# Hybrid encoder layer: both merge gates as seven block products behind the heads, triangular inverses without DRAM, outputs of a head in a tile of their own, decays refilled step by step

## The chip, the cores and the metric

The kernel runs on one core of one Trainium2 chip. The metric is the device time of one execution in microseconds (us). Three runs of the kernel before gave 1963.44, 1961.55 and 1962.57 us. The profile is of one execution more; its times count from that execution's first instruction.

Engines are named as in the profile: PE is the matrix engine (PEld its weight loads), DVE the vector engine, ACT the scalar engine, POOL the engine GpSimd, SP the engine that issues nearly all DMAs. L332 is line 332 of the kernel before.

## The reference, cut to what matters

One layer over 1040 tokens (16 learned tokens ahead of 1024), width 1024, all in float32:

```python
h = rmsnorm(h_res, norm1_w)
proj = h @ w_in                                   # 9248 columns
(q, k, v, z, b_raw, a_raw, sc_b, sc_c, sc_x, gate_a, gate_b) = split(proj)
o_dn = gated_deltanet_bidir(q, k, v, z, b_raw, a_raw, ...)   # 8 heads, forward and backward scan
y_a = o_dn @ w_branch_dn
y_b = (sc_b * dwconv3(sc_c * sc_x)) @ w_branch_sc
merged = sigmoid(gate_a) * y_a + sigmoid(gate_b) * y_b
h_res += merged @ w_out
h_res += (silu(gu[:, :FF]) * gu[:, FF:]) @ w_down            # gu = rmsnorm(h_res) @ w_gate_up
out = rmsnorm(h_res)
```

A head of the delta net works on chunks of tokens. In each chunk and direction it needs the inverse of a unit triangular matrix (beta times k k^T times a decay), and then a recurrent step: the state S of 128x128 goes from chunk to chunk, forward in one direction, backward in the other.

## The kernel before, in words

**Matmuls.** Each float32 operand is split into a high and a low part (`split`, L85), and a product is three matmuls: high x high, high x low, low x high. A full product of w_in's 128 columns with all tokens ("a unit") is 48 matmuls with 512 columns each (two halves, eight k steps, three matmuls: `dense_steps`, L324), or 72 shorter ones in three pieces of 336 (or 322), 320 and 384 columns.

**The heads' stage.** Up to about 985 us, PE works through units: 24 for q, k, v of the eight heads, 8 for z, 24 for the short convolution (columns C, X, B; `u_short`, L417) and 7 for gate B (`u_gate`, L450). `pick` (L923) chooses the next: q, k, v first if `qkv_ok` allows, else the next of the list `fill_units`. A chosen unit runs two units later (list `ahead`), its weights are loaded and split meanwhile. `qkv_ok` (L919) holds a head back until `near` (a count that the scan of an earlier head raises when it starts step NEAR = 3) and `nscan` (scans begun) allow it. The first unit of a head, its k, waits in `u_qkv` (L378) after its first piece until the scan three heads before has ended (`freed`), since it takes that head's buffer.

**The streams.** Between the steps of the units, `run_streams` (L967) advances the generators of the heads' chain, and `pump` (L301) issues DVE work of four lanes (`conv`, `short`, `fs`, `norm`). All of it is one order written out ahead by a planner that keeps estimated clocks T of PE, DVE, ACT and POOL; the engines then run that order, each in order. For head h:

- `g_decay` (L514): one DMA broadcasts the head's row of decays into PQ (16 tiles of 128x128, two buffers), then a mask is added (L522) and ACT takes exponentials (L527). It may start when the scan of head h-2 has ended (`freed`).
- `g_norm` (L531): transposes and norms of q and k; then, when the scan of h-2 is wholly done (`done`, and `stored` some time after it), k k^T and q k^T for each chunk (L583), times the decays into NP (L613) and PQ (L617). NP has two buffers.
- `g_inv` (L623): the 32x32 diagonal blocks of NP go out to DRAM (nd, L641) and come back in another layout into fN (L653); `fs_job` (L484) inverts them by forward substitution, 62 DVE operations in a row (L491, L495); the result goes out to DRAM (pd, L671) and back into NP (L676). With the lock taken (`take`, L509), ACT copies and DVE transposes (L687 to L697) and matmuls of blocks follow (L706 to L741). The 16x16 matrix of the learned tokens is inverted meanwhile on POOL on one partition (L661).
- `g_scan` (L745): under the same lock it scales v (L764), and after the inverse 8 steps (L796 to L873). The outputs are gathered in parts of NP (`oacc`, L773), normalised, transposed and stored (L899, L902) after the lock is given back.

One lock serves the scan and the second part of the inverse. One generator of each kind runs at a time.

**Behind the heads.** `ph1.close()` frees the stage's memory, and the tiles of the next stage are allocated in it. One unit of gate B is made by `dense` (L1427), then gate A, the short convolution's projection and the delta net's projection each by `seven` (L1367): a product of 2x2 blocks by seven block products, each of 4 k steps, 4 tiles and 3 matmuls, so 7 x 48 = 336 matmuls (L1382) in place of 8 x 48 = 384. The sums of blocks of the hidden states (T1 to T4) are made late in the heads' stage (`block_sums`, L271) and kept in DRAM. The gates' tanh values go to DRAM (ta_d, tb_d) and come back at the merge.

**At the start.** POOL makes triangular masks (L1178 to L1196) in memory of their own while PE still makes the first units. The pool `dn` (L1298) takes over the memory of the start's pool `st`; `g_gates` (L1202) then uses the masks in PE matmuls (L1266, L1278).

## Time and profile before

| | us |
|---|---|
| median of three runs | 1962.57 |
| lowest, highest | 1961.55, 1963.44 |
| span of the profiled execution | 1959.4 |
| last matmul of the heads' stage begins (L332) | 985.2 |
| the one dense unit behind it | 985.4 to 996.5 |
| first matmul of `seven` (L1382) | 996.5 |
| output projection begins (L1596) | 1225.0 |
| gate and up projection begins (L1656) | 1318.4 |
| down projection begins (L1813) | 1742.0 |

The page gives for each engine its busy time and share of the span, then the span in 40 slices, then the chain of work that ended last, followed backwards. Further views group instructions by line (times in ns for one), print them in order of time, or sum them up over a stretch. A matmul's end is modelled, so the distance between the starts of matmuls, not their durations, tells the rate. An idle time in square brackets is followed by what ended it.

### The profile page before, as it was taken

The page shows a single profiled execution, that of the slowest core. Times are in us where ns is not written, and L with a number is a line of the kernel's source. Part 1 is how long each engine was busy: PE and PEld are TensorE (multiplying, and loading weights), DVE is VectorE, ACT ScalarE, POOL GpSimd, SP SyncE. Part 2 cuts the span into 40 slices and gives each one's busy share as a digit, 9 for nine tenths or more (in the row PEclk, how much of TensorE's full clock was granted, in tenths as well). Part 3 has the DMA queues.
Part 4 walks back from the last instruction along what each step waited for, and adds up shares of the span by engine and source line. Part 5 has one row for each costly group of instructions (what it writes and reads, how often), then busy time and mean ns, then how long its engine had stood idle before and what let it go on. Part 6 is the DMA issues. An engine that isn't in the chain of part 4 may idle for free.

```text
span 1959.4 us, 31938 instructions
## 1 busy us (share of the span) xinstructions
PE 1941.7 (99%) x11962; PEld 1704.4 (87%) x11962; DVE 1468.1 (75%) x2804; ACT 867.9 (44%) x2014; POOL 158.4 (8%) x457
## 2 busy tenths in 40 slices
PE   8999999999999999999999999999999999999998
PEld 8998899999899999998888888887888888888887
DVE  4778778788887888787358798559787887756574
ACT  5463544646455554533445545234232332324343
POOL 3012112020110202110000000000000000000001
PEclk9999999999999999999999999999999999999999
DMA  4222332323222222224386623332666644587654
GB/s 146 68 76 80 103 99 60 87 60 87 60 76 67 85 65 79 70 69 153 103 310 246 206 88 121 115 119 73 212 232 209 209 165 163 179 279 243 194 181 155
DMA packets 243136, 264.11 MB, mean 135 GB/s; under 512 B 46820, under 2 KB 166933, under 8 KB 240549
## 3 DMA queue, kind: packets, MB, share of 16 engines
q1 hardware_dynamic: 242981, 262.07, 42.1%
q8 instruction: 94, 1.54, 0.3%
q14 instruction: 61, 0.50, 0.1%
HBM read 189.58 MB, written 72.44 MB: 134 GB/s over the span
## 4 chain that ended last, share of the span: by engine, by line
PE 89%; DVE 5%; ACT 3%; issue 1%; DMA 1%; POOL 0%; SPq 0%; POOLq 0%; DVEq 0%; ACTq 0%
PE pm L332 31%; PE pm L1382 5%; PE pd L1382 4%; PE pe L1382 3%; PE pm L1656 3%; PE pm L1658 3%; PE pm L1657 2%; PE pd L1658 2%; PE pd L1656 2%; PE pd L1657 2%; PE pe L1658 2%; PE pe L1656 2%; PE pe L1657 2%; PE pm L1814 1%; PE pm L1815 1%; PE pm L1813 1%
## 5 line engine op out<-in xcount | busy, mean ns | idle before, releaser
L332 PE MATMUL pm<-hTh,wh 128*128 128x512 f32 (+4 forms) x1328 | 483.8, 365 | 0.1
L332 PE MATMUL pm<-hTh,wl 128*128 128x512 f32 (+4 forms) x1328 | 450.5, 340 | 0.0
L332 PE MATMUL pm<-al,wh 128*128 128x512 f32 (+4 forms) x1328 | 449.6, 339 | 0.5 <-DVE al L1047 0.5
L332 PEld LDWEIGHTS pm<-hTh,wl 128*128 128x128 f32 x1328 | 249.1, 188 | 15.5
L332 PEld LDWEIGHTS pm<-hTh,wh 128*128 128x128 f32 x1328 | 250.2, 189 | 13.6 <-ACT hTh L1041 0.2
L332 PEld LDWEIGHTS pm<-al,wh 128*128 128x128 f32 x1328 | 250.4, 189 | 12.9 <-DVE al L1047 0.7
L87 DVE TENSOR_TENSOR al<-raw,ring_h 128x1024 fp32r<-128x1024 f32 x73 | 88.4, 1223 | 63.6 <-ACT ring_h L86 63.2
L86 ACT CAST ring_h<-raw 128x1024 fp32r<-128x1024 f32 x73 | 76.9, 1054 | 109.7 <-PE pd L1815 35.3
L940 DVE TENSOR_TENSOR wl<-raw,wh 128x512 fp32r<-128x512 f32 x122 | 84.1, 690 | 32.0 <-ACT wh L943 27.1
L355 DVE SCALAR_TENSOR_TENSOR kq<-ra,wc,kq 128x520 f32<-128x520 f32 (+1 forms) x128 | 95.9, 749 | 2.3 <-ACT kq L389 1.2
L821 ACT ACTIVATE w<-pd,small 128x128 f32<-128x128 f32 x128 | 40.2, 365 | 124.9 <-PE pd L814 106.4
L128 POOL TENSOR_SCALAR ss<-ss 128x1 f32<-128x1 f32 x13 | 4.6, 353 | 951.1 <-ACT b L1825 603.4
L491 DVE TENSOR_TENSOR tm<-fP,fN 128x135 f32<-128x135 f32 (+23 forms) x248 | 72.1, 291 | 10.0 <-DMA fN<-nd 3.3
L495 DVE TENSOR_TENSOR fP<-fP,tm 128x135 f32<-128x135 f32 (+23 forms) x248 | 71.8, 289 | 7.3
L943 ACT CAST wh<-raw 128x512 fp32r<-128x512 f32 x122 | 74.8, 619 | 0.1
L87 DVE TENSOR_TENSOR raw<-pair,raw 128x1024 fp32r<-128x1024 f32 (+1 forms) x42 | 48.0, 1143 | 30.4 <-ACT raw L86 30.4
L86 ACT CAST raw<-pair 128x1024 fp32r<-128x1024 f32 (+1 forms) x42 | 41.7, 992 | 58.4 <-PE pd L1382 27.5
L87 DVE TENSOR_TENSOR wl<-pair,wh 128x1024 fp32r<-128x1024 f32 (+1 forms) x42 | 48.1, 1144 | 21.7 <-ACT wh L86 21.6
L86 ACT CAST wh<-pair 128x1024 fp32r<-128x1024 f32 (+1 forms) x42 | 41.7, 992 | 46.0 <-PE pd L1382 24.7
L843 DVE SCALAR_TENSOR_TENSOR S<-S,eGl,pd 128x128 f32<-128x128 f32 x104 | 31.8, 344 | 38.2 <-PE pd L831 30.8
L130 POOL TENSOR_TENSOR small<-small,minus_half 128x9 f32<-128x9 f32 x16 | 29.5, 1842 | 353.8 <-DVE small L878 264.0
L661 POOL TENSOR_TENSOR tm<-mP,mN 1x15 f32<-1x15 f32 (+7 forms) x120 | 37.3, 311 | 237.0 <-DMA mN<-ndm 228.7
(660 smaller groups left out, 4945.7 us busy)
## 6 DMA issues: line engine op xcount, KB each, us to landing
raw<-in_w_in_dram SPq DMA_DIRECT2D x64, 512.0 KB
raw<-in_w_gate_up_dram SPq DMA_DIRECT2D x44, 512.0 KB
sums<-in_w_down_dram SPq DMA_DIRECT2D x22, 512.0 KB
t_d<-sums SPq DMA_DIRECT2D x11, 1024.0 KB
raw<-s_d SPq DMA_DIRECT2D x44, 256.0 KB
raw<-t_d SPq DMA_DIRECT2D x44, 256.0 KB
act_d<-b SPq DMA_DIRECT2D x43, 256.0 KB
raw<-act_d SPq DMA_DIRECT2D x33, 256.0 KB
```

Source lines behind the costliest of these rows:

```text
L86: nc.scalar.copy(hi, src)
L87: nc.vector.tensor_tensor(out=lo, in0=src, in1=hi.bitcast(F32), op=ALU.subtract)
L332: mm(po[:, :n], (wl if j == 2 else wh)[:, k], xl[k][:, t0:t0 + n] if j == 1 else xh[k][:, t0:t0 + n], start=(i == 0), stop=(i == 3 * KT - 1))
L355: nc.vector.scalar_tensor_tensor(out=acc, in0=raw[:, h0 + t:h0 + t + hn], scalar=wc[:, t, col:col + 1], in1=acc, op0=ALU.mult, op1=ALU.add)
L491: nc.vector.tensor_tensor(out=tv, in0=fP[:, 0:r, j:j + 1].broadcast_to([P, r, n]), in1=fN[:, j:j + 1, j + 1:32].broadcast_to([P, r, n]), o ...
L495: nc.vector.tensor_tensor(out=fP[:, 0:r, j + 1:32], in0=fP[:, 0:r, j + 1:32], in1=tv, op=ALU.subtract)
L940: nc.vector.tensor_tensor(out=u[1][1][:, k], in0=u[2][:, k], in1=u[1][0][:, k].bitcast(F32), op=ALU.subtract)
L943: nc.scalar.copy(u[1][0][:, k], u[2][:, k])
L1382: mm(bank[t], a[:, c], b, start=fresh, stop=first and k == 3 and j == 2, skip_group_check=not first)
L1656: mm(po, ah[:, k], bhk, start=k == 0, stop=False)
L1657: mm(po, ah[:, k], blk, start=False, stop=False)
L1658: mm(po, al[:, k], bhk, start=False, stop=k == 3)
```

## The change

Both gates leave the heads' stage. Its fill list ends with seven of the eight B units of the short convolution; the eighth is made by `dense` behind the heads, in the place of gate B's eighth unit. Then `seven` runs for gate B and for gate A. So `seven` now runs four times. The results of the short convolution's taps (yc) go through DRAM to the late B units.

```diff
     fill_units += [(off + j * P, lambda w, j=j, i=i: u_short(j, i, w), None, i)
-                   for j in range(8) for i, off in enumerate((OSC, OSX, OSB))]
-    gates = [(j, off, d_[j]) for off, d_ in ((OGB, tb_d), (OGA, ta_d)) for j in range(8)]
-    late = gates[max(0, len(gates) - LATE):]
-    fill_units += [... u_gate(j, d_, w) ... for j, off, d_ in gates[:len(gates) - LATE]]
-    NEAR = 3
+                   for j in range(8) for i, off in enumerate((OSC, OSX))]
+    fill_units += [(OSB + j * P, lambda w, j=j: u_short(j, 2, w), None, None) for j in range(7)]
+    NEAR = 1
...
+    w = wload(w_in, OSB + 7 * P)
+    yc = s4(SEQ)
+    nc.sync.dma_start(yc, yc_d[7])
+    for i in range(2):
+        po = psany()
+        dense(po, w, hx, C0 + META + 512 * i, 512)
+        nc.vector.tensor_tensor(out=yc[:, halves[i]], in0=po, in1=yc[:, halves[i]], op=ALU.mult)
+        front.pop(0)()
+    nc.sync.dma_start(p_d[7], yc)
...
-    seven(ga, bank_m, bank_d, (0, 1), evict_ga, during_ga, ...)
+    for d, X, Y, dst, during in ((gb, bank_m, bank_d, tb_d, during_gb), (ga, bank_d, bank_m, ta_d, during_ga)):
+        seven(d, X, Y, (0, 1), evict_gate(dst), during, ...)
```

`during_gb` loads the blocks of w_in and T1 to T4 for gate A while gate B's products run, as `during_ga` does for the projection after it; the two sets of PSUM banks change places from one `seven` to the next.

The decays are refilled slot by slot. PQ and NP become two fixed tiles each; slot i of PQ holds the forward chunk i and the backward chunk 7 - i, the two that step i of the scan uses.

```diff
+        def fetch(i):
+            for d, c in enumerate((i, NC - 1 - i)):
+                nc.sync.dma_start(PQ[:, i, d], grow[h:h + 1, c, d].broadcast_to([P, P]))
+            return T["pe"] + ARRIVE          # ARRIVE is 5000 ns now, it was 10000
+        for i in range(NC + 1):
+            while i < NC and h > 1 and heads[h - 2]["steps"] <= i:
+                yield T["pe"] + 100
...
-        while done < h - 1 or "PQ" not in st_:
-        if h > 1:
-            yield heads[h - 2]["stored"]
+        while "PQ" not in st_:
+        order = (3, 4, 2, 5, 1, 6, 0, 7)     # chunks, as the slots that they need come free
...
-        oacc = [NP[:, c, c // 4] for c in range(NC)]
+        O = dn.tile([P, NC, P], F32, tag="o", name=uid("o"))
+        oacc = [O[:, c] for c in range(NC)]
...
-        if h < H and h < freed + 2 and not decs:
+        if h < H and h < freed + 3 and not decs and (h < 2 or "steps" in heads[h - 2]):
-        if ... h < freed + 3 and not norms and ...
+        if ... h < scaled_heads + 3 and not norms and ...
```

The inverse's blocks no longer go through DRAM. ACT copies them together (four copies of 32x512), two DVE transposes bring them into the layout of `fs_job` (256 and 1024 columns), and two more (512 columns each) bring the result back. The rows of a block are spread over two groups of partitions so that each operation of `fs_job` has j // 2 + 1 rows instead of up to 16. The copies of finished blocks into NP (`diag`, 32x256 on ACT) stand between the matmuls of the second part.

```diff
-            r = min(j + 1, 8) if j < 16 else 8 + min(j - 15, 8)
+            r = j // 2 + 1
...
+            nc.scalar.copy(E[B(b)].rearrange("p d c i -> p c d i"), NP[B(b), :, :, B(b)])     # for b in range(4)
+        nc.vector.transpose(E[:, 0], E[:, 0])
+        nc.vector.transpose(fN.rearrange("p i (s x) -> p i s x", s=2),
+                            E.rearrange("p d c i -> p i (d c)").unsqueeze(2).broadcast_to([P, 32, 2, 2 * NC]))
         job = enqueue("fs", fs_job(h, fN, fP))
...
+        nc.vector.transpose(Z.rearrange("p d c r -> p r (d c)"), fP.rearrange("p r (s x) -> p (r s) x", s=2))
+        nc.vector.transpose(W, Z)
         yield from take("inv")
```

The learned tokens' matrix gets a generator of its own, `g_meta`, on 16 partitions of POOL, begun as soon as the matrix is there; the scan waits for it (`learned`). The triangular masks of the start are now made in the first NP buffer, so behind the allocation of the pool `dn`, and `g_gates` puts its rows rr there too.

More of the change, by code (lines that the diff above doesn't have):

```diff
@@ L28 @@
 NF = FF // P
-LATE = 9
 EPS = 1e-6
@@ L179, in encoder_layer @@
     p_d = [dr.tile([P, SEQ], F32, name=f"p_d{i}") for i in range(KT)]
+    yc_d = [dr.tile([P, SEQ], F32, name=f"yc_d{i}") for i in range(KT)]
     ta_d = [dr.tile([P, SEQ], F32, name=f"ta_d{i}") for i in range(KT)]
@@ L654, in g_inv @@
[L654 to L665 removed]
+        fPf = fP.rearrange("p r i -> p (r i)")
@@ new lines, in g_inv @@
+        nc.gpsimd.memset(fP, 0.0)
+        nc.gpsimd.memset(fPf[:, 1:512:34], 1.0)
+        for b in range(4):
+            even = fPf[32 * b:32 * b + 16]
+            nc.gpsimd.memset(even[:, 1:512:34], 0.0)
+            nc.gpsimd.memset(even[:, 0:512:34], 1.0)
+        on("pool", 1500)
+        for b in range(4):
+            nc.scalar.copy(E[B(b)].rearrange("p d c i -> p c d i"), NP[B(b), :, :, B(b)])
+            A(512)
+        yield T["act"] + HOP
+        nc.vector.transpose(E[:, 0], E[:, 0])
@@ L767, in g_scan @@
         yield T["act"] + HOP - 1000
-        while not st_.get("inverted"):
+        while not (st_.get("inverted") and st_.get("learned")):
             yield T["pe"] + 100
@@ L952, in start_streams @@
         h = nnorm
-        if h < H and ndec and h < freed + 3 and not norms and all(k in heads[h] and heads[h][k]() for k in ("tk", "tq")):
+        if h < H and ndec and h < scaled_heads + 3 and not norms and all(k in heads[h] and heads[h][k]() for k in ("tk", "tq")):
             norms.append([g_norm(h, heads[h]), T["dve"] + HOP, h])
             nnorm += 1
+        h = nmeta
+        if h < H and not metas and heads[h].get("Nm_done"):
+            metas.append([g_meta(h, heads[h]), T["dve"] + HOP, h])
+            nmeta += 1
         h = ninv
@@ L1422, in encoder_layer @@
-    for j, off, dst in late[:len(late) - 8]:
-        w = wload(w_in, off + j * P)
-        th = s4(SEQ)
-        for i in range(2):
-            po = psany()
-            dense(po, w, hx, C0 + META + 512 * i, 512)
-            nc.scalar.activation(th[:, halves[i]], po, AF.Tanh, scale=0.5)
-            if front:
-                front.pop(0)()
-        nc.sync.dma_start(dst, th)
+    w_gate = {"a": w_in[:, OGA:OGA + D], "b": w_in[:, OGB:OGB + D]}
+    gb = {k: pair(t) for k, t in zip("ABCDEG", ("b0", "b1", "b2", "b3", "mB", "mA"))}
```

380 lines of the change are left out of this document (185 added, 195 removed).

## The prediction

> **What bounds the kernel now.** I began with the page's shares and slices, then summed the engines by stretch.
>
> ```profile
> span 1959.4 us, 31938 instructions
> PE 1941.7 (99%) x11962; PEld 1704.4 (87%) x11962; DVE 1468.1 (75%) x2804; ACT 867.9 (44%) x2014; POOL 158.4 (8%) x457
> PEclk9999999999999999999999999999999999999999
> 30.00:985.00 955.00, 951.09 (x7475) 882.62 (x7476) 740.27 (x1883) 481.06 (x1513) 131.45 (x402) 1.00 0.28 80
> 997.00:1226.00 229.00, 229.00 (x1010) 189.24 (x1009) 189.86 (x206) 117.61 (x145) 0.00 (x0) 1.00 0.57 196
> ```
>
> The last two rows are stretches: length, then busy us of PE, PEld, DVE, ACT and POOL, granted clock, DMA share, GB/s. The first is the heads' stage, the second the three runs of `seven`. PE is without work for 4 us of 955 in the one and for none in the other, at full clock. So PE's queue bounds both, and an edit counts by the matmuls that it takes out and by the waits that it puts into PE's order. The rate, from the chain that ended last (start, length, what):
>
> ```profile
> 996.47 2.04 PE pm L1382 x9
> 1018.23 2.04 PE pm L1382 x9
> L455 ACT ACTIVATE rb<-pm x14: 578/598/617, 892.1 to 985.7; 128x512 f32<-128x512 f32 x14
> L741 ACT COPY NP<-pd x8: 581/582/584, 211.2 to 901.0; 64x512 f32<-64x512 f32 x8
> ```
>
> Two block products, 96 matmuls, lie between the first two rows: 21.76 / 96 = 0.2267 us for a matmul of 512 columns. L455 evicts gate B's units, two halves each: seven units stand at the very end of the heads' stage. L741 ends a head's inverse, and its first and last start give (901.0 - 211.2) / 7 = 98.5 us per head. So the heads' chain, not PE, sets how early the stage could end if its fill were taken away, and that is what the change does. Here is one turn of this chain, from the end of head 5's scan to that of head 7:
>
> ```profile
> 765.43 0.60 PE L834 MATMUL pd<-v,PQ 128*128 128x128 f32 x4
> 800.66 0.69 ACT L527 ACTIVATE PQ<-PQ,negG 128x128 f32<-128x128 f32 x2
> 816.77 0.42 DVE L617 TENSOR_TENSOR PQ<-pe,PQ 128x256 f32<-128x256 f32 x1
> 820.01 1.83 DVE L639 STREAM_TRANSPOSE NP<-NP 32x256 f32<-32x256 f32 x4
> 836.94 0.18 DVE L491 TENSOR_TENSOR tm<-fP,fN 128x31 f32<-128x31 f32 x1
> 872.37 0.19 DVE L495 TENSOR_TENSOR fP<-fP,tm 128x16 f32<-128x16 f32 x1
> 885.47 0.41 ACT L687 COPY Xe<-NP 32x256 f32<-32x256 f32 x1 [2.97 <-DMA meta_inv<-pdm]
> 901.02 0.58 ACT L741 COPY NP<-pd 64x512 f32<-64x512 f32 x1
> L777 PE MATMUL pd<-vS,meta_inv x16: 270/273/275, 214.7 to 903.9; 128*128 128x128 f32 x16
> 903.84 0.38 PE L777 MATMUL pd<-vS,meta_inv 128*128 128x128 f32 x2
> 961.57 0.60 PE L834 MATMUL pd<-v,PQ 128*128 128x128 f32 x4
> ```
>
> The decays take 35 us after scan 5 (to 801.3), the products 16 (817.2), the way out through DRAM and back 15 (821.8 to 836.9), the substitution 35.6, the second way through DRAM 12.9 (872.6 to 885.5), the inverse's second part 16.1 (to 901.6), the scan 58.3 (903.8 to 962.2). That is 196 us for two heads, 98 for one, and agrees with L741.
>
> **Gate B's matmuls.** A dense gate is 8 x 48 = 384 matmuls of 512 columns, `seven` 336. 48 go: 48 x 0.2267 = **-10.9 us**. The eight units that leave the heads' stage (seven of gate B, the eighth B unit) are 8 x 48 x 0.2267 = 87.1 us, the new `seven` is 336 x 0.2267 = 76.2 us, and the dense unit between stays. PE's work of the heads' stage then ends at 985 - 87.1 = 898 us. The -10.9 holds only if the chain is done by then; from 898 each us of lateness is a us lost, and at 908.8 nothing is left.
>
> **The chain after.** With slots fetched as scan h-2 steps, about 12 us are left behind its last step: one fetch (5 us by the planner), mask and exponentials 1.1, two chunks' products about 2 (rows L527, L617), hops. The first DRAM way becomes four ACT copies (0.58 each by L741) and two transposes (0.46 by L639's mean for 256 columns, perhaps 1.3 for 1024), some 6 us; the second becomes two transposes and hops, some 3. These shapes are not in the trace; were each as dear as the whole of what it replaces, 15 and 13 us would stay. The substitution keeps 62 operations with 24% fewer elements, 2856 in place of 3752 in a pass:
>
> ```profile
> L491 DVE TENSOR_TENSOR tm<-fP,fN 128x135 f32<-128x135 f32 (+23 forms) x248 | 72.1, 291 | 10.0 <-DMA fN<-nd 3.3
> L495 DVE TENSOR_TENSOR fP<-fP,tm 128x135 f32<-128x135 f32 (+23 forms) x248 | 71.8, 289 | 7.3
> L940 DVE TENSOR_TENSOR wl<-raw,wh 128x512 fp32r<-128x512 f32 x122 | 84.1, 690 | 32.0 <-ACT wh L943 27.1
> 500.00:600.00 100.00, 100.00 (x833) 95.75 (x833) 88.22 (x231) 53.30 (x176) 16.90 (x53) 1.00 0.26 72
> ```
>
> At 1.07 ns an element (L617's 256 columns take 0.42 us, L491's 31 take 0.18) that is about 1.9 us of 18 per head; say 33 us for the 35.6. The second part loses seven transposes and gains copies beside matmuls: 14 for 16.1. The turn is then 12 + 6 + 33 + 3 + 14 + 58 = 126, 63 per head. But the second part and the scan share the lock: 14 + 58 + some 8 for vS and hand-overs = **80 us a head**, and this binds. Head 0's first scan starts near 198 (L777's first start is 214.7; less two DRAM ways of some 10, plus the 3 below); its end is near 255, that of head 7 at 255 + 7 x 80 = 815, its outputs stored at 827. PE's 898 comes 71 us later: the period may be 90 before PE waits. DVE can stretch it. In the densest stretch (last row) it has 88.2 of 100 us. In the stage it falls from 740 us by 8 x 1.38 (units' splits, two of L940 each), 8 x 1.9 (substitution) and about 8 x 1.7 (11 transposes of 0.46 against four of 3.3 in all) to some 700 in 868, 81%, but nearer 90 until the chain ends. So I take 84 to 86 as likely, an end near 860, and count the chain at nothing. What covers it is the B units' work after 860; with that cover gone it costs what the rival below says.
>
> **The start.** The masks move behind the allocation of `dn`.
>
> ```profile
> 37.88 0.20 POOL L1178 MEMSET Uf<- 128x128 f32 x1
> 43.32 0.30 POOL L1196 TENSOR_SCALAR mask<-Ub 128x128 f32<-128x128 f32 x1
> 53.43 0.35 POOL L1301 MEMSET meta_inv<- 128x128 f32 x2 [9.82 <-PE pe L1053]
> 54.55 0.37 ACT L1223 COPY scratch<-pe 128x256 f32<-128x256 f32 x1 [0.67 <-PE pe L83]
> 54.95 0.42 DVE L1227 TENSOR_TENSOR scratch<-pe,scratch 128x256 f32<-128x256 f32 x1 [3.44 <-ACT scratch L1223]
> 71.42 0.51 DVE L1258 TENSOR_TENSOR scratch<-scratch,alg 128x64 f32<-128x64 f32 x4
> 73.29 0.34 PE L1266 MATMUL pe<-scratch,U2f 128*128 128x72 f32 x2
> ```
>
> POOL spends 5.7 us on them (37.9 to 43.6) while nothing waits. The first memset in `dn` could start only at 53.4, when PE had read the last tile of `st`. The masks now go ahead of it in POOL's order, and the memset of scratch that L1223 overwrites comes behind: L1223 moves from 54.5 to about 60.2. Queued behind it on ACT are a split of weights and the eviction of v's first piece, which catch up by 64; behind it on DVE all of `g_gates`. DVE has slack of about 1.8 us in ACT's way, then runs without a gap, so L1258 ends near 76, and PE, whose order has L1266 at 73.3, waits about 3 us. **+3.0**, between 0 (DVE catches up) and 5.7 (no slack).
>
> **A head's k unit.** NEAR goes from step 3 to step 1. For head 7, which waits for scan 4:
>
> ```profile
> 619.09 0.61 PE L796 MATMUL pd<-S,kq 128*128 128x128 f32 x4
> 633.84 0.60 PE L796 MATMUL pd<-S,kq 128*128 128x128 f32 x4
> 663.43 0.60 PE L834 MATMUL pd<-v,PQ 128*128 128x128 f32 x4
> 683.90 0.43 ACT L388 COPY ra<-pm 128x336 f32<-128x336 f32 x1
> ```
>
> These are steps 1 and 3 of scan 4, its last step, and the first piece of k 7. From step 3 the piece came after 50 us, long after the scan's end. From step 1 it would come at 669, 5 us after the end (664). Two units lie between choice and start, and where in a unit (14.4 us by L455's 14 halves in 93.6 us, longer beside a scan) the choice falls shifts it by some 7 us either way, so one head in three may meet the wait at L378, for a few us. PE then has only the scan's matmuls, a third of its time. I take **+2.0** for the five heads; nothing at best, at worst 7 us x 5 with 60% idle, 20 us.
>
> **The hand-over behind the heads.**
>
> ```profile
> 988.48 2.29 SPq L1346 DMA_DIRECT2D pair<-in_w_in_dram  x4
> 993.70 0.62 ACT L86 CAST raw<-pair 128x512 fp32r<-128x512 f32 x1 [1.98 <-DMA pair<-in_w_in_dram]
> ```
>
> SP can load into the new tiles from 988.5. The first split stands at 993.7, 2.8 us before L1382 starts. The load of yc (512 KB) goes ahead now and takes about 2 us of this slack; the last product evicted goes through DVE (0.68) rather than ACT. **+0.5**, 0 to 2. Gate A's blocks, the late B units' yc and the fetches (16 a head at 0.34 us on SP, where some 19 DMAs of the inverse go) come early enough: SP has no place on the chain now. Between gate B and gate A the banks and buffers turn over as between gate A and the projection now, where PE lost nothing.
>
> **Sum.** 1959.4 - 10.9 + 3.0 + 2.0 + 0.5 = 1954.0 of span. The runs' median lies 3.2 us above the profiled span, and I add that: **1957.2, say 1957 us**.
>
> **Rivals.**
> 1. *The chain ends too late; slower.* The place is the lock, or DVE at its limit. The price: at a period of 93 us head 7's scan ends at 906, its outputs at 918, 20 us past PE's work: 1957 + 20 = 1977. It costs more than it gives from a period of about 91.6 (908.8). At the present 98.5 it would be some 2015. For it speaks DVE's 88.2; against it the 28 us of DRAM ways and 39 of 51 us before the inverse that go from a turn.
> 2. *Given back inside the heads' stage.* The denser order meets more waits: k units at L378, row buffers whose convolutions DVE has not done. 4 to 10 us above my sum: 1961 to 1967, take 1964. For: scan 4 took 45 us from step 1 to its end, and k 7 came 50 us after its choice became free, less up to 7. Against: 4 us idle in 955 with the same planner.
> The Trainium skill ("TensorE: Matmul & The Clock Gate", the section on the clock gate) says that PE's clock falls to half after an idle window of about 3.4 us; by that a wait at L378 of that length would, by an estimate from this page, cost up to 1.7 us more (half of 3.4 until the clock is back). Here the clock is 1.00 in every stretch, and no run shows such a gap.
> 3. *The stage also loses its small waits.* 4 us of idle PE and part of the start go: 1949.
>
> **Chances.** Forecast 0.55 (1950 to 1960), given back 0.24, slower chain 0.15, further gain 0.06. A difference under 0.2%, 3.9 us, cannot be told from none. The forecast lies 5.6 under the median, near that bound: 0.47 of its 0.55 is faster. With the further gain faster is 0.53; same 0.27 (0.08 and 0.19 of rival 2); slower 0.20 (0.05 and 0.15). The range runs from 1949 to 1970, which leaves out the worse half of the late chain and the far end of rival 2.
>
> **What would show it.** Right: L1382 with 1344 matmuls and no gap, 305 us; the last L332 near 903; the last L899 before it, and L777's starts some 80 to 86 us apart; L1266 late by 3 us; no gap of PE after a k unit's first piece. Wrong: L899 after the last L332; idle PE in the middle of the stage; a wait at the first split behind the heads.

## The result, and the profile after

| | before | after |
|---|---|---|
| median of four runs, us | 1963.01 | 1994.62 |
| lowest, highest | 1961.55, 1963.63 | 1992.65, 1996.39 |
| profiled span | 1959.4 | 1993.9 |

The ratio is 1.0162, with a 95% interval of 1.0147 to 1.0176: the change costs 32 us, where 6 were to be gained. Line numbers of "after" are those of the changed kernel. Its page begins so:

```profile
span 1993.9 us, 32160 instructions
## 1 busy us (share of the span) xinstructions
PE 1945.6 (98%) x11914; PEld 1700.9 (85%) x11914; DVE 1479.4 (74%) x2812; ACT 937.0 (47%) x2142; POOL 173.5 (9%) x497
```

The matmuls went as promised, 11962 to 11914, 48 fewer. But PE was busy for 99% and is now for 98% of a longer span. Sums over stretches of after (length, then busy us of PE, PEld, DVE, ACT and POOL with their instructions, granted clock, DMA share, GB/s): the heads' stage to its last dense matmul, the same to the first block product, and the two new `seven` with the projection's two:

```profile
30.00:925.00 895.00, 869.55 (x7059) 810.14 (x7060) 697.17 (x1822) 507.60 (x1569) 144.84 (x441) 1.00 0.24 70
30.00:950.00 920.00, 885.21 (x7141) 822.64 (x7141) 708.94 (x1845) 513.91 (x1591) 146.65 (x442) 0.99 0.25 74
950.00:1260.00 310.00, 308.76 (x1344) 253.59 (x1344) 234.58 (x255) 157.25 (x201) 0.00 (x0) 0.99 0.55 190
```

And the same stretch of before, from 30 us to its first block product:

```profile
30.00:996.00 966.00, 962.09 (x7523) 891.75 (x7524) 741.86 (x1886) 483.93 (x1518) 131.45 (x402) 1.00 0.29 81
```

Length less PE's busy time is PE's idle time: 966 - 962.1 = 3.9 us before, 920 - 885.2 = **34.8 us** after. Of these, 895 - 869.6 = 25.4 lie in the stage itself, the rest behind its last dense matmul (the stage of before, 30 to 985 us, had 3.9). What PE waited for in after (total, times, longest), by the view of PE's waits from 30 to 950 us:

```profile
PE pm L1390 <- ACT raw L85: 8.5, 1, 8.5
PE pe L588 <- DVE PQ L626: 8.2, 6, 2.8
PE pd L821 <- DVE r L813: 4.2, 5, 1.2
PE pe L82 <- DVE Nm L571: 2.9, 4, 1.4
```

The first is the hand-over: the first block product stands behind a split whose block could be loaded only after head 7's outputs had left the stage's memory. The others are steps of the heads' chain (the products k k^T, the scan) that wait for DVE. What such a wait looks like, first PE, then DVE, in order of time (start, length; in brackets the idle time before, and what ended it):

```profile
483.71 0.34 PE L331 MATMUL pm<-hTh,wl 128*128 128x384 f32 x1
486.83 0.70 PE L588 MATMUL pe<-kq 128*128 128x256 f32 x2 [2.77 <-DVE PQ L626]
```

```profile
478.47 0.59 DVE L620 SCALAR_TENSOR_TENSOR NP<-pe,small,PQ 128x128 f32<-128x128 f32 x2
478.98 1.53 DVE L354 SCALAR_TENSOR_TENSOR vT<-ra,wc,vT 128x520 f32<-128x520 f32 x2
481.22 0.70 DVE L362 SCALAR_TENSOR_TENSOR vT<-rb,vT 128x520 f32<-128x520 f32 x1 [0.70 <-ACT rb L359]
481.84 3.14 DVE L354 SCALAR_TENSOR_TENSOR vT<-ra,wc,vT 128x520 f32<-128x520 f32 x4
485.68 0.76 DVE L362 SCALAR_TENSOR_TENSOR vT<-rb,vT 128x520 f32<-128x520 f32 x1 [0.70 <-ACT rb L359]
486.36 0.41 DVE L626 TENSOR_TENSOR PQ<-pe,PQ 128x256 f32<-128x256 f32 x1
```

A chunk's product (L626) comes 7.3 us after the operation before it in the chain (L620, done at 479.1), with a convolution in between, as `row_buffer` forces it out when the next unit needs a buffer. PE's queue holds the next chunk's matmul (L588), which needs the bank that L626 reads, and the dense work stands behind it. What follows costs more, in stretches of 1 us:

```profile
487.00:488.00 1.00, 1.00 (x6) 0.95 (x7) 0.97 (x2) 0.96 (x3) 0.89 (x2) 1.00 0.02 8
488.00:489.00 1.00, 1.00 (x6) 1.00 (x5) 0.97 (x4) 0.95 (x4) 0.72 (x4) 0.61 0.29 31
489.00:490.00 1.00, 1.00 (x5) 1.00 (x4) 1.00 (x3) 0.96 (x4) 0.82 (x3) 0.50 0.96 253
490.00:491.00 1.00, 1.00 (x5) 1.00 (x4) 1.00 (x4) 0.96 (x3) 0.82 (x3) 0.50 0.83 249
491.00:492.00 1.00, 1.00 (x4) 0.72 (x3) 1.00 (x4) 0.76 (x2) 0.92 (x2) 0.68 0.00 0
```

Some 1.4 us after PE took up work again its clock falls to half for 3.4 us, which costs half of that, 1.7 us. This happens twice in the stage; a third and longer fall goes with the hand-over.

And the chain's pace, by the line of a scan's first matmul (shortest, median, longest in ns; first and last start):

```profile
L784 PE MATMUL pd<-vS,meta_inv x16: 270/273/275, 206.1 to 875.4; 128*128 128x128 f32 x16
L841 PE MATMUL pd<-v,PQ x256: 270/275/377, 216.9 to 931.9; 128*128 128x128 f32 x128
```

(875.4 - 206.1) / 7 = 95.6 us a head. Before it was 98.5. The last scan matmul is at 931.9, 7 us behind the last dense matmul of the stage.

### The profile page after: what moved, and what is told of

The parts are those of the page before. It is cut to its first block, busy times and chain, and to the rows that moved or that the text cites. A ratio compares the mean times of both kernels' runs of the same rounds, so it can differ in the third digit from the quotient of the medians.

```text
span 1993.9 us, 32160 instructions
## 1 busy us (share of the span) xinstructions
PE 1945.6 (98%) x11914; PEld 1700.9 (85%) x11914; DVE 1479.4 (74%) x2812; ACT 937.0 (47%) x2142; POOL 173.5 (9%) x497
## 4 chain that ended last, share of the span: by engine, by line
PE 58%; DVE 4%; ACT 2%; DMA 1%; issue 1%; POOL 0%; POOLq 0%; SPq 0%; ACTq 0%; DVEq 0%
PE pm L331 6%; PE pm L1390 5%; PE pd L1390 5%; PE pe L1390 4%; PE pm L1676 3%; PE pm L1677 3%; PE pm L1675 3%; PE pd L1675 2%; PE pd L1677 2%; PE pd L1676 2%; PE pe L1675 2%; PE pe L1676 2%; PE pe L1677 2%; PE pm L1833 1%; PE pm L1834 1%; PE pm L1832 1%
## 5 line engine op out<-in xcount | busy, mean ns | idle before, releaser
L331 PE MATMUL pm<-hTh,wh 128*128 128x384 f32 (+4 forms) x1200 | 433.9, 363 | 0.1
L331 PE MATMUL pm<-hTh,wl 128*128 128x384 f32 (+4 forms) x1200 | 402.2, 336 | 0.0
L331 PE MATMUL pm<-al,wh 128*128 128x384 f32 (+4 forms) x1200 | 401.0, 335 | 0.5 <-DVE al L1057 0.5
L331 PEld LDWEIGHTS pm<-hTh,wh 128*128 128x128 f32 x1200 | 227.1, 190 | 9.2 <-ACT hTh L1051 0.2
L331 PEld LDWEIGHTS pm<-hTh,wl 128*128 128x128 f32 x1200 | 226.1, 189 | 10.3
L331 PEld LDWEIGHTS pm<-al,wh 128*128 128x128 f32 x1200 | 227.3, 190 | 8.4 <-DVE al L1057 0.7
L86 DVE TENSOR_TENSOR al<-raw,ring_h 128x1024 fp32r<-128x1024 f32 x73 | 88.4, 1222 | 64.3 <-ACT ring_h L85 64.1
L485 DVE TENSOR_TENSOR tm<-fP,fN 128x126 f32<-128x126 f32 (+22 forms) x248 | 62.9, 254 | 6.9
L489 DVE TENSOR_TENSOR fP<-fP,tm 128x126 f32<-128x126 f32 (+22 forms) x248 | 62.7, 253 | 6.7
L1345 DVE TENSOR_TENSOR b<-pm,b 128x512 f32<-128x512 f32 x65 | 43.6, 684 | 21.7 <-PE pm L1677 19.0
L85 ACT CAST mB<-raw 128x1024 fp32r<-128x1024 f32 x24 | 25.1, 1052 | 69.8 <-DVE raw L140 53.6
L532 ACT ACTIVATE PQ<-PQ,negG 128x128 f32<-128x128 f32 x128 | 44.2, 394 | 26.4 <-DVE PQ L528 26.1
```

What stands on the lines that cost most here:

```text
L85: nc.scalar.copy(hi, src)
L86: nc.vector.tensor_tensor(out=lo, in0=src, in1=hi.bitcast(F32), op=ALU.subtract)
L331: mm(po[:, :n], (wl if j == 2 else wh)[:, k], xl[k][:, t0:t0 + n] if j == 1 else xh[k][:, t0:t0 + n], start=(i == 0), stop=(i == 3 * KT - 1))
L485: nc.vector.tensor_tensor(out=tv, in0=fP[:, 0:r, j:j + 1].broadcast_to([P, r, n]), in1=fN[:, j:j + 1, j + 1:32].broadcast_to([P, r, n]), o ...
L489: nc.vector.tensor_tensor(out=fP[:, 0:r, j + 1:32], in0=fP[:, 0:r, j + 1:32], in1=tv, op=ALU.subtract)
```

## The experiments

In what follows "the first block product" is the start of the first `seven`, and each row is the stretch from 30 us to there unless the text says otherwise. "The stage" ends with its last dense matmul (L331 in after). Length less the second number is PE's idle time. The medians of the kernel before in these series were 1961.7 to 1963.4 us; a ratio is to those runs.

### One half of the change at a time

**Gates only**: the kernel before with the fill list, the late SB unit and the four `seven` of after. The late B units load yc one half at a time, not both ahead. The chain is untouched.

```diff
-    fill_units += [... u_gate ... for j, off, d_ in gates[:len(gates) - LATE]]
+    fill_units += [(OSB + j * P, lambda w, j=j: u_short(j, 2, w), None, None) for j in range(7)]
...
+    for d, X, Y, dst, during in ((gb, ...), (ga, ...)):
+        seven(d, X, Y, (0, 1), evict_gate(dst), during, ...)
```

> The kernel before with one part of the change: both gates by seven block products behind the heads (and one SB unit there), the heads' chain as it was before (inverse through DRAM, decays in one piece after the scan, NEAR 3). Theory 'fill' (the 95 to 98 us per head are the chain's own time, and the thinner fill lays it bare): scans stay 98 us apart, the stage ends near 980 as before although PE has 87 us less to do, PE idles 60 to 80 us in it, 2020 to 2040 us. Theory 'queue' (a head's 95 to 98 us are PE's own instructions in their queue, and the stalls of the change come from the new chain's instructions): scans about 88 apart, PE idle 4 to 8 us in the stage, 10.9 us of matmuls gone and a hand-over of about 10 to 15 at the end: 1960 to 1970 us.

**Chain only**: the kernel after with the gates as before.

```diff
-    fill_units += [(OSB + j * P, lambda w, j=j: u_short(j, 2, w), None, None) for j in range(7)]
+    fill_units += [... u_gate ... for j, off, d_ in gates[:len(gates) - LATE]]
```

> The kernel after with the gates as before (seven units of gate B as fill in the heads' stage, the eighth and one of gate A behind it... that is, gate B dense, gate A by seven), so the new chain alone (inverse without DRAM, own tile for the outputs, decays refilled during the scan, masks made late, NEAR 1). Theory 'fill': the fill covers the chain again, PE idle in the stage near 4 us, 1960 to 1966 us (the late masks cost 2). Theory 'queue': the 20 us of PE idle that the changed kernel shows in the middle of the heads' stage (products and scan steps waiting for DVE) are here as well, 1978 to 1990 us.

Measured: gates only 2013.02 us, 1.0253 [1.0238, 1.0268]; chain only 1984.46 us, 1.0107 [1.009, 1.0124]. A row of each, gates only first, there also a row for the stage alone, and the line of a scan's first matmul:

```profile
30.00:969.00 939.00, 895.43 (x7141) 831.39 (x7142) 732.42 (x1868) 468.12 (x1487) 133.10 (x402) 0.98 0.29 83
30.00:880.00 850.00, 839.82 (x6686) 786.52 (x6687) 684.39 (x1775) 440.38 (x1396) 131.29 (x401) 1.00 0.29 81
L770 PE MATMUL pd<-vS,meta_inv x16: 270/273/377, 214.8 to 900.8; 128*128 128x128 f32 x16
```

```profile
30.00:1021.00 991.00, 972.55 (x7525) 897.16 (x7526) 721.63 (x1864) 533.05 (x1624) 147.03 (x442) 0.99 0.24 69
L789 PE MATMUL pd<-vS,meta_inv x16: 270/272/275, 207.5 to 898.6; 128*128 128x128 f32 x16
```

The old chain keeps its 98 us a head, (900.8 - 214.8) / 7, when the fill is thinned: in this 'fill' holds for it, though PE idles for 43.6 us where that theory had 60 to 80, and the time lies below its 2020 to 2040. In the stage the idle time is 10.2 us; the other 33 lie behind it, where the last scan is still under way. Taking the gates out alone costs 50 us. The new chain alone costs 21 us although the fill is as thick as before, with PE idle for 18.5 us, all in the stage: 'queue' holds for it. Under that fill its scans are 98.7 us apart, (898.6 - 207.5) / 7.

So the stalls in the stage of after come for the larger part with the new chain: over the 3.9 us of before, the chain alone brings 14.5 us and the thin fill alone 6.3, together 20.8, and after has 21.5. Behind the stage it is the other way round: the new chain ends sooner after the fill than the old one, and so takes back 18 of the 50 us.

**Decays late**: of the chain's parts, only the refill during the scan is undone.

```diff
-            while i < NC and h > 1 and heads[h - 2]["steps"] <= i:
+            while i < NC and h > 1 and heads[h - 2]["steps"] < NC:
```

> The kernel after without one part of the change: a head's decays are fetched only when the scan two heads before is done with all its steps, not chunk by chunk as it frees them (memory and order of the products as in the kernel after). If the refill during the scan is what loads DVE and ACT beside the scan and so makes PE's stalls: idle 10 to 15 instead of 25 in the heads' stage, 1975 to 1985 us. If it is what shortens the chain: scans 100 us apart, 2005 to 2020 us. If it does neither: 1990 to 1998 us.

1991.43 us, and the last scan begins at 874.8 instead of 875.3 us, with the first at 207.6: 95.3 a head. The refill does not shorten the chain, and at most a small part of the stalls is its own (PE idles for 31.5 instead of 34.8 us). The inverse without DRAM and the tile of the outputs were not tried by themselves.

**NEAR 3** in after, as before (`NEAR = 1` becomes `NEAR = 3`):

> The kernel after with NEAR 3 instead of 1: the k unit of head h + 3 may be taken two scan steps later, as before. Theory 'late k units' (units wait for kq buffers, ACT for row buffers): the waits at the k units go, but the last q and v units and so the last scans come 5 to 10 us later: idle of PE 20 to 25, time 1990 to 2005 us. Theory 'lumps': no part in it, time within 5 us of 1994.

1999.20 us, 5 us slower than after, as 'late k units' had it: PE idles for 20.7 us in the stage instead of 25.4, but the last scan begins 13 us later (888.7 against 875.4). So the earlier choice of k units brings some waits and is a gain all the same.

### Load, length, or order

**Splits on POOL**: the low part of each weight split leaves DVE, in after and, as a control, in before.

```diff
-            nc.vector.tensor_tensor(out=u[1][1][:, k], in0=u[2][:, k], in1=..., op=ALU.subtract)
+            nc.gpsimd.tensor_tensor(out=u[1][1][:, k], in0=u[2][:, k], in1=..., op=ALU.subtract)
```

> The kernel after, with the second half of each weight split (the low part, raw minus high, 128x512, 106 of them at 0.685 us = 72 us of DVE in the heads' stage) on POOL, which is busy for about 160 us of the 900; everything else as it is. Theory 'DVE's load' (with the thinner fill a head has 87 us of DVE in 95, so a late convolution or substitution can't be caught up, and PE's queue runs into it): 72 us less on DVE, idle of PE in the heads' stage from 25 to under 12, the stage's last dense matmul 10 to 18 earlier, the scan's end no longer last, no or a short hand-over gap: 1962 to 1978 us. Theory 'order alone' (the lumps of forced convolutions are what is late, whatever the load): idle 20 and more, 1988 to 1996 us. Against it: POOL needs about 1.3 us for such a piece, and the rsqrt of a head's norms waits behind it, which could cost up to 1 us per head.

> The kernel before with the low parts of the splits on POOL, as a control. There PE idles for 4 us only, so nothing is to be had from DVE: all theories 1958 to 1966 us. If it is much faster, the gain of split_pool says nothing on the change.

2018.07 and 1987.25 us, both some 24 us worse than without. So this run can't tell what it was made for. Two groups of DVE, by shape, from 30 to 925 us, show that the load on DVE was not lowered; after first, then splits on POOL:

```profile
L354 DVE SCALAR_TENSOR_TENSOR kq<-ra,wc,kq 128x520 f32<-128x520 f32 x96 | 72.2, 753 | 1.1
L354 DVE SCALAR_TENSOR_TENSOR vT<-ra,wc,vT 128x520 f32<-128x520 f32 x64 | 47.9, 749 | 1.1
```

```profile
L354 DVE SCALAR_TENSOR_TENSOR kq<-ra,wc,kq 128x520 f32<-128x520 f32 x96 | 79.1, 824 | 1.7 <-ACT kq L388 0.5
L354 DVE SCALAR_TENSOR_TENSOR vT<-ra,wc,vT 128x520 f32<-128x520 f32 x64 | 57.6, 900 | 1.1
```

The same convolution step takes 0.82 to 0.90 us instead of 0.75 when the splits are on POOL. The Trainium skill ("GPSIMD Engine Reference", the section on specifications) says that POOL shares its ways to the memory with DVE and contends with DVE instructions that have two inputs there; the trace agrees, with these longer steps. Where PE lost the 24 us was not taken apart.

**Two taps** and **half the substitution** take work off DVE without putting it anywhere. The first leaves out two of the four taps that DVE adds in each convolution, the second every other step of the substitution.

```diff
-            for t in (0, 1, 3, 4):
+            for t in (1, 3):
```

```diff
-        for j in range(31):
+        for j in range(0, 31, 2):
```

> The kernel after, leaving out two of the four taps that each convolution has on DVE: 96 operations of 0.75 us, 72 us less on DVE in the heads' stage (as much as the low parts of the splits, and nothing put on POOL, whose work slowed DVE's convolutions from 0.75 to 0.82 to 0.90 us in split_pool). Of the chain's own path it shortens only the q convolution, by 3 us per head. Theory 'DVE's load': scans 84 to 88 us apart instead of 95.6, idle of PE in the heads' stage under 12 us, no hand-over gap, 1955 to 1968 us. Theory 'serial chain': 3 us per head at most, scans 92 apart, 1975 to 1985 us.

> The kernel after, leaving out every second step of the forward substitution: 31 of 62 dependent operations per head, 63 us of DVE in all, and about 17 to 20 us less per head on the chain's own path. Theory 'DVE's load': as taps2, within 5 us. Theory 'serial chain': much more than taps2, scans 78 to 82 us apart, and PE left with fill for the end: 1950 to 1958 us.

1986.84 us (1.0127) and 1983.82 us (1.0111). Two taps first:

```profile
30.00:944.00 914.00, 888.17 (x7141) 829.95 (x7142) 639.21 (x1747) 513.32 (x1592) 136.63 (x442) 0.99 0.25 75
L784 PE MATMUL pd<-vS,meta_inv x16: 270/272/275, 208.1 to 849.3; 128*128 128x128 f32 x16
```

```profile
30.00:940.00 910.00, 885.52 (x7140) 823.44 (x7141) 651.55 (x1603) 512.61 (x1592) 142.43 (x442) 0.99 0.25 75
L784 PE MATMUL pd<-vS,meta_inv x16: 270/272/275, 193.6 to 812.3; 128*128 128x128 f32 x16
```

DVE has 70 and 57 us less to do than in after (708.9), the scans come 91.6 and 88.4 us apart instead of 95.6, the hand-over gap is gone, and yet PE idles for 25.8 and 24.5 us, all of it in the stage, as much as in the stage of after (25.4). The two lie within 5 us of each other, as 'DVE's load' had it, but far above the 1955 to 1968 us that it gave; 'serial chain' had the scans of two taps right (92 us) and its time nearly (1975 to 1985), but not half the substitution (78 to 82 us apart, 1950 to 1958). A faster chain removes the wait at the hand-over; the idle time in the stage stays.

**Order alone.** The remaining kernels change only the planner's rules: all have the 11914 matmuls and 2812 DVE operations of after, but for one with the splits on POOL as well and a control made from the kernel before. First, which job DVE takes when a convolution and a substitution step are both ready. In *conv first* any convolution goes first; in *conv next* only that of the head to be inverted next.

```diff
             k = min(cand, key=lambda q: spent[q])
+            if "conv" in cand and lanes["conv"][0].head <= ninv:     # conv next; conv first has no second condition
+                k = "conv"
```

> The kernel after, with one line of the rule that orders DVE's work: a convolution that is ready goes ahead of a substitution step, instead of behind a whole substitution (its account is far below that of the convolutions, so that it always wins). Theory 'lumps' (PE's stalls follow from convolutions that are forced out in one piece of 3 to 7 us on DVE when a row buffer is needed): PE idle in the heads' stage falls from 25 to 10 to 15 us, 1980 to 1985 us. Theory 'DVE's total' (77% busy, so any order is late somewhere) or 'latency of the chain': idle stays at 20 to 30, 1990 to 2000 us.

> The kernel after with only that order (convolutions of the next head first, those of later heads behind the substitution), splits on DVE. Theory 'order': as good as conv_first or better, 1972 to 1984 us, since the first head's substitution isn't delayed (conv_first's first scan began 25 us late). Theory 'DVE's load': what a convolution gains a substitution loses, 1980 to 1995 us.

> As split_pool, and with the convolutions of the head that is next to be inverted ahead of the running substitution (others behind it, as before). If load and order are two separate causes, this is faster than each alone: split_pool less 8 to 12 us, 1950 to 1968 us. If it is the load alone, as split_pool within 4 us. If the order alone, near 1982 as conv_first.

1982.27, 1981.35 and, conv next with the splits on POOL too, 1985.18 us. The first came out as 'lumps' had it, in its time and in its idle time in the stage, 14.3 us (10 to 15 expected, 25.4 in after); another 11.3 us lie behind the stage, since the chain ends last. Conv next lies where both of its theories had it. The last agrees with 'order alone', its scans 87.3 us apart and PE idle for 25.5 us all the same. The stage of conv first, then that of conv next and its whole stretch:

```profile
30.00:906.00 876.00, 861.66 (x7030) 804.55 (x7031) 690.45 (x1814) 504.53 (x1554) 152.67 (x441) 1.00 0.25 73
30.00:892.00 862.00, 854.35 (x6980) 799.04 (x6981) 681.41 (x1791) 499.82 (x1540) 145.02 (x441) 1.00 0.25 73
30.00:937.00 907.00, 882.09 (x7141) 821.54 (x7141) 702.51 (x1844) 513.45 (x1590) 146.82 (x442) 0.99 0.26 75
```

In the stage of conv next only 7.7 us of idle are left, but the scans still come 94.4 us apart, and the last ends 28 us after the fill's last matmul (919.7 against 892.0 us): another 17.3 us idle, at the end.

*FS close* lets the substitution's steps follow each other closely, *FS close, conv* adds conv next.

```diff
-            yield T["dve"] + DEP          # 127
+            yield T["dve"] + 60           # both places in fs_job
```

> The kernel after with one number of its planner: the gap that it leaves behind each substitution step, 60 ns instead of 127 (the trace has 20 to 40 ns between dependent steps where nothing stands between them). So fewer other operations are put between the steps; DVE's work is the same. Theory 'DVE's load': within 6 us of 1994, since the load is the same. Theory 'order' (the substitution takes 36 to 45 us for 15.7 us of work because 0.7 us operations stand between its steps): the substitutions take 20 to 28 us, scans 85 to 90 apart, 1965 to 1980 us.

> fs_close and conv_next together: substitution steps close together, convolutions of the next head before them. Theory 'order': scans 82 to 87 us apart, dense matmuls left when the last scan ends, no hand-over gap, PE idle 8 to 14 us in the heads' stage: 1948 to 1962 us, level with the kernel before or faster. Theory 'DVE's load': the chain's end stays near 930, 1975 to 1985 us.

1986.19 us, in the range of neither theory, and 1974.83 us. The second:

```profile
30.00:932.00 902.00, 882.67 (x7141) 824.21 (x7142) 700.34 (x1843) 513.27 (x1591) 151.34 (x442) 0.99 0.26 75
L787 PE MATMUL pd<-vS,meta_inv x16: 270/273/275, 206.5 to 809.9; 128*128 128x128 f32 x16
```

Its chain is as fast as I had forecast, 86.2 us a head, and is done 55 us before the stage. Even so PE idles 19.3 us, where 'order' had 8 to 14.

From there two edits give PE's dependent instructions a later place. *Hop 600*: `TOPE = 600` instead of 370 in fs close, conv. *Product late*, also in fs close, conv:

```diff
             pk, t = nxt or kkq(c)
             nxt = None
-            if n + 1 < NC and ready(order[n + 1]):
-                nxt = kkq(order[n + 1])
             yield max(t, st_["exp"][c, 0], st_["exp"][c, 1])
             ...                                              # the two products into NP
             yield T["dve"] - 200
+            if n + 1 < NC and ready(order[n + 1]):
+                nxt = kkq(order[n + 1])
```

> fs_close_conv with one more number of the planner: 600 ns instead of 370 between the end of an operation on DVE or ACT and the place in PE's queue of what needs it. DVE's and ACT's work and their order by rule are the same. Theory 'early' (the planner reckons DVE and ACT too fast, 0.26 us for a 128-column operation that took 0.34, so PE's dependent instructions stand in PE's queue before their data are there; the old chain's long waits for DRAM hid that): PE idle in the heads' stage falls from 19 to under 10, scans 88 to 90 us apart instead of 86, still fill left at the last scan: 1960 to 1967 us. Theory 'conserved' (the idle is the chain's latency and only moves): idle in the middle less, the same again at the end: 1972 to 1980 us.

> fs_close_conv with one edit at the products: the next chunk's matmul is issued behind the two products on DVE that read the last one, not ahead of them. PE's longest waits in fs_close_conv (7.4 us at this matmul, for the product before last) then have 0.7 us more room. Theory 'early': those 7 us go, 1966 to 1970 us. Theory 'conserved': they turn up at another line, 1972 to 1978 us.

Hop 600 took 1969.03 us, between the two theories, with 16.9 us of idle. Product late took **1960.22 us, a ratio of 0.9995 [0.9984, 1.0007]** to before, below both theories. Its stage, its scans, and its block products:

```profile
30.00:916.00 886.00, 877.24 (x7143) 820.50 (x7144) 699.61 (x1845) 516.45 (x1593) 150.54 (x442) 1.00 0.26 77
L787 PE MATMUL pd<-vS,meta_inv x16: 270/273/377, 198.8 to 805.3; 128*128 128x128 f32 x16
916.00:1224.00 308.00, 305.39 (x1342) 250.95 (x1341) 234.39 (x255) 155.66 (x199) 0.00 (x0) 1.00 0.56 190
```

PE idles 8.8 us, the clock is whole, scans are 86.6 us apart. This is the changed kernel, every instruction of it, 34 us faster by order alone.

Three kernels ask whether that order can be explained: the last edit alone in after, the three edits in before, and product late with hop 600.

> The kernel after with only the edit at the products (the next chunk's matmul behind the two products), the order of convolutions and the gap of the substitution as in the kernel after. If that one place is the cause, it is near prod_late: 1960 to 1968 us. If the three edits act together (DVE's order brings the chain's end forward, the products' place takes PE's waits away): the 11 us of waits at the products go, the chain still ends last with the hand-over gap, 1978 to 1988 us.

> The kernel before with the same three edits of order as prod_late, as a control. PE idles 4 us of its heads' stage, its chain ends behind nothing but fill, so there is nothing to gain but those 4: 1958 to 1964 us. If it comes out under 1955, prod_late's gain is the edits' own and says nothing on the change.

> prod_late with 600 ns instead of 370 before PE's dependent instructions, the last of the orders that the theory 'early' asks for. prod_late's chain ends 27 us before its fill does, so there is room for 2 to 3 us per head. By 'early' the 8 us of PE idle left in the middle fall to 3 to 5: 1954 to 1959 us, and with it the change made well is faster than before by 0.2 to 0.4%. By 'conserved' 1960 to 1964 us.

2004.73, 1971.63 and 1979.14 us: none where a theory had put it. The edit that takes 15 us off fs close, conv adds 10 to after. Hop 600 takes 6 off fs close, conv and adds 19 to product late. And the order edits cost the kernel before 10 us (1961.88 in the same series). Rows of product late alone, of product late with hop 600, and of the kernel before with the order edits:

```profile
30.00:960.00 930.00, 891.35 (x7140) 828.84 (x7141) 710.00 (x1845) 514.03 (x1591) 141.58 (x442) 0.99 0.25 73
```

```profile
30.00:935.00 905.00, 879.88 (x7139) 822.68 (x7140) 699.29 (x1843) 513.64 (x1591) 148.61 (x442) 1.00 0.25 75
```

```profile
30.00:1004.00 974.00, 961.98 (x7523) 892.05 (x7524) 738.29 (x1886) 483.46 (x1518) 142.08 (x402) 1.00 0.29 81
```

All kernels with the changed kernel's instructions, by PE's idle time from 30 us to the first block product:

| kernel | idle, us | scans apart, us | median, us |
|---|---|---|---|
| product late | 8.8 | 86.6 | 1960.2 |
| hop 600 | 16.9 | 88.9 | 1969.0 |
| FS close, conv | 19.3 | 86.2 | 1974.8 |
| conv next | 24.9 | 94.4 | 1981.4 |
| product late with hop 600 | 25.1 | 90.5 | 1979.1 |
| conv first | 25.6 | 90.6 | 1982.3 |
| FS close | 26.3 | 93.5 | 1986.2 |
| decays late | 31.5 | 95.3 | 1991.4 |
| after | 34.8 | 95.6 | 1994.6 |
| NEAR 3 | 36.7 | 97.3 | 1999.2 |
| product late alone | 38.7 | 97.7 | 2004.7 |

The time follows the idle time: 44.5 us for 29.9 us of idle, 1.5 us for each. Of the half beyond the idle itself, the half clock that follows a stall is the larger part: over the same matmuls PE is busy 14.1 us longer in product late alone than in product late (891.35 and 877.24), and its clock is at half for some 20 us of the stage of the first and never in that of the second, which makes about 10 of the 14.

## Why the prediction was wrong

The prediction was 1957 us, between 1949 and 1970; it came to 1994.6.

**The matmuls taken out (-10.9): right.** 48 fewer matmuls. Block products were to take 305 us without a gap; they took 309.9 (949.9 to 1259.8), 308.7 in product late. The 4 to 5 us were not in the sum. In after some 3 us of it come from the half clock in the first 6 us; PE's idle time is 1.2 us.

**The late masks (+3.0): too high.** PE waited 1.1 us there.

**The k units (+2.0): wrong sign in all.** With NEAR 3 PE idles 4.8 us less in the stage of after, so there are such waits, but the kernel is 5 us slower, since the chain comes later.

**The hand-over (+0.5): wrong in after**, 8.5 us, since the chain ended last. In product late, where it did not, the first block product came 11.1 us after the stage's last dense matmul, which is the dense unit itself.

**The step that failed is "count the chain at nothing".** I took 84 to 86 us a head, bound by the lock, and an end near 860; it was 95.6 us and an end near 932. But the period was only half of it. I had added up the chain's steps and PE's matmuls apart from each other, and held that PE waits only if the chain ends after 898. The runs show that PE loses time before the chain is late: at 86.2 us a head, with the chain done 55 us early, it still idled 19 us (FS close, conv), and with half the substitution gone 24.5. Each step of the chain has matmuls in PE's queue at a place fixed beforehand, and where DVE or ACT is late at such a place the dense work behind it waits too. The missing term was PE's idle time in the heads' stage. Without any new wait the first block product would begin at 909.4 (996.5 less 87.1); the sum put 5.5 us of waits on top (3, 2 and 0.5) and so had it at 915, and it came at 949.9. Of these 40.5 us, 30.9 are idle time of PE (34.8 against 3.9) and some 3.4 the half clock in the stage; what the other 6 are, in which PE counts as busy, is not shown. The three signs of being wrong that the prediction named all came: output work behind the stage's last dense matmul, idle PE in the middle, a wait at the first split behind the heads.

**The rivals.** Rival 1 gave 1977 us at a period of 93 and 2015 at 98.5, which is 1995 at 95.6, the time measured. That is mostly luck. The late chain is a part only, the 8.5 us of the hand-over (gates only is the kernel that loses by it, 33 us behind its stage); more is lost in the stage, and kernels with a fast chain lose there too: half the substitution and product late with hop 600 have periods of 88.4 and 90.5 us, at which it has next to no cost, and took 1984 and 1979 us, and FS close, conv took 1975 at 86.2. Neither the lock nor DVE's load was shown to set the time: 70 us less on DVE brought 8 us. Rival 2 had the place, row buffers whose convolutions DVE has not done, as at 479 to 486 us, and gave it 4 to 10 us, where PE's idle time in the stage rose from 4 to 25. I took the 4 us idle of before for a property of the planner. It was a property of that order: three edits of order that leave the kernel's work as it was made it 12.

**The sum came out in one order.** In product late the first block product came at 915.5 us, the dense work ended at 904.4 (forecast 898 to 903), the scans were 86.6 us apart, and the span was 1958.3 against 1954.0, the difference being the 4 us of the block products. As the small terms did not come out one by one, their total (5.5, where PE's idle time rose by 4.9) agrees in part by luck.

**What stays open.** That the order of the same instructions moves the time by up to 44.5 us is shown. Which rule makes a good order is not: that PE's dependent instructions stand too early ('early') has the direction of hop 600 and product late, though not their times, and fails in product late with hop 600 and product late alone. The edits don't add up: conv next and FS close give 13 and 8 us, together 20; with product late, which alone costs 10, they give 34. No version was faster than the kernel before by more than the runs can tell: product late lies 2 us below it, inside its interval.

## What to carry to other kernels

When one engine is busy for 99% under an order written out ahead, its small idle time belongs to that order. A change to the other engines' work draws a new order, and the spread between orders (some 45 us here) can be larger than the gain (10.9 us). So before judging such a change, try it with several orders. In a prediction, give the new waits of the full engine a term of their own, sized by the idle time of other orders, not by that of the tuned kernel. And test two parts of a change in all four combinations: here each part alone lost (50 and 21 us), and both together lost less than the sum.

## What the runs showed of the hardware

**The clock.** The prediction quoted the Trainium skill ("TensorE: Matmul & The Clock Gate", the section on the clock gate) for half clock after an idle window of about 3.4 us. Here it followed a gap of 2.77 us (rows of 487 to 492 us), with the fall some 1.4 us after work had begun again; the half clock itself lasted 3.4 us. It followed another gap of 2.29 us, which ended at 763.9 us, by 0.8 us, while one of 2.29 us that ended at 165.4 was not followed by it:

```profile
764.00:765.00 1.00, 1.00 (x8) 1.00 (x9) 0.90 (x5) 0.97 (x6) 0.00 (x0) 0.85 0.00 0
765.00:766.00 1.00, 1.00 (x5) 1.00 (x5) 0.88 (x4) 0.94 (x7) 0.00 (x0) 0.50 0.00 0
...
166.00:167.00 1.00, 1.00 (x6) 0.82 (x5) 1.00 (x4) 0.49 (x2) 0.00 (x0) 1.00 1.11 178
167.00:168.00 1.00, 1.00 (x6) 0.79 (x6) 0.96 (x5) 0.53 (x2) 0.00 (x0) 1.00 0.55 67
```

In chain only the clock fell at 586.3 us behind two waits of 1.15 and 0.91 us close together (they ended at 584.15 and 585.3). So the length of one gap does not settle it, and these traces don't show what does.

**DVE's transposes.** I had put the transpose of 1024 columns at perhaps 1.3 us, and the four of a head at 3.3. In after they take 2.05, 1.12, 0.70 and 0.44, together 4.3; of two with 512 columns, the one that writes its columns in another order (L681) takes 1.12 us and the plain one (L684) 0.70:

```profile
L669 DVE STREAM_TRANSPOSE fN<-E x8: 2016/2048/2086, 147.5 to 808.5; 128x1024 f32<-128x1024 f32 x8
L681 DVE STREAM_TRANSPOSE XT<-fP x8: 1086/1122/1164, 187.1 to 851.7; 128x512 f32<-128x512 f32 x8
L684 DVE STREAM_TRANSPOSE W<-XT x8: 680/698/712, 188.3 to 854.5; 128x512 f32<-128x512 f32 x8
```

**POOL beside DVE.** (The row is the stage of splits on POOL.) An operation moved to POOL is not free for DVE: 144 us of subtractions there made DVE's convolution steps 9 to 20% longer, and its busy time in the stage fell from 708.9 us to 708.0 only, of 72 that had been taken off:

```profile
30.00:974.00 944.00, 896.85 (x7140) 832.26 (x7141) 707.98 (x1738) 514.39 (x1592) 284.12 (x548) 0.98 0.24 72
```
